# Dilated values with tokens in rows: a stage of their own, two of three head groups by seven block products, read back by class order from DRAM

## The chip, the core and the metric

The kernel runs on one core of one Trainium2 chip. The time is the device time of one execution in microseconds (us). Three runs of the kernel before took 1468.01, 1468.41 and 1469.43 us; their median, 1468.41 us, is what the new time is compared with. A core has five engines that take their instructions in order, each from its own queue: TensorE (PE in the profile, its weight loads PEld), VectorE (DVE), ScalarE (ACT), GpSimd (POOL) and SyncE (SP). SP issues most DMAs here, ScalarE's queue some.

## What is computed

The reference is one layer of an encoder: a normalised input of 1024 tokens x 1024 channels, three mixers beside each other, gates, and an output projection.

```python
h = rms_norm(x, g_pre)
a_qkv, bq, bk, bv, mq, ga, gb, gm, mg = split(h @ w_in)
# A: dilated sliding windows, 3 groups of 8 heads of 64, (window, dilation) = (128,1), (512,4), (2048,16)
aq, ak, av = rope(a_q, pos), rope(a_k, pos), a_v
for gi, (window, dil) in enumerate(A_GROUPS):     # keys and queries regrouped by token % dil
    o_g, lse_g = dilated_window_attention(aq[gi], ak[gi], av[gi], window, dil)
oa = sum over groups of softmax(lse)[g] * o_g
# B: grouped-query attention (8 heads, 2 key heads), M: cross-attention into 256 memory rows
ya, yb, ym = (oa * silu(ga)) @ w_br_a, (ob * silu(gb)) @ w_br_b, (om * silu(gm)) @ w_br_m
merged = sigmoid(mg0)*ya + sigmoid(mg1)*yb + sigmoid(mg2)*ym
out = x + rms_norm(merged @ w_out, g_post)
```

The change concerns `av`, the values of the dilated mixer: 3 groups x 8 heads x 64 = 1536 columns of `h @ w_in`, for 1024 tokens.

## The kernel before

Every large product is made in float32 by three passes of a split operand: `x = xh + xl`, `w = wh + wl`, and `xh*wh + xl*wh + xh*wl`. The input, transposed, stays in SBUF as eight pairs `hh[k]`, `hl[k]` (channels k in partitions, tokens along the row). `split` (L104) makes a pair: ScalarE copies the high part, VectorE subtracts it.

A *unit* is 128 columns of `w_in` for all tokens. `load_w` (L110) loads its 512 KB into one of two `wr` tiles from SP and splits it into one of two pairs `wh`, `wl`; `add_unit` (L195) puts it in a queue: for each half of the tokens 24 matmuls (8 k x 3 passes, lines L143, L145, L147 of `dense`) into one of two PSUM banks `d`, and then an evacuation that frees the bank. The weights stand still, the tokens move, so a unit's result has channels in partitions and tokens along the row. `weave` (L174) merges the matmuls of the queue with the instructions of an attention in one order for TensorE, which is written out by hand; each attention piece has a cost, and pieces and matmuls advance in proportion to what is left. A piece's own instructions come after its cost has been spent in matmuls, so the last piece of an attention item comes behind all matmuls woven with that item. In the stages spoken of here the orders of VectorE, ScalarE, GpSimd and SP are set by a planner of the framework, from priorities and its own costs; some stages fix those by hand too (`manual_schedule`).

The order of the work: the input is split and the cross-attention is made; then the grouped-query attention with gate units woven in (`b_att`); then the dilated stage (PSUM phase `ps_a`); then the 22 merge-gate units that are left, by a block scheme with seven products per pair (phase `ps_w`); then the branch products and the output projection.

The dilated stage works on 12 items, head pairs p = 0..3 by groups g = 0..2, in the order (0,0), (0,1), (0,2), (1,0) and so on. Each item has three units: query, key, value (`add_a`, L869; the very first item has them in the order value, key, query). Queries and keys are rotated by `rope_half` (L851): four VectorE products of 32 partitions into `t2a`, one of 128 into `t1a` (L860, L861), and a GpSimd sum (L867) that also writes tokens regrouped by class (token % dilation). The value evacuation (L892) multiplies by the inverse norm into `vta`, by class too; GpSimd copies the half blocks at the ends of a class into `vda` (L898). While an item's attention runs, the units of the next item are woven in: `weave(3, ...)`.

The attention of an item (`item`, L904; `plan`, L1066) has eight token tiles T of 128 queries. In the order of `plan`: scores of tiles 0 to 3 come at the end of the item before, behind its first half product with the values (`joined(it["pv"][0], nxt["scores"][0])`); softmax of a tile is VectorE's masked minimum (L960) and ScalarE's exponentials; TensorE transposes the weights (L985, L994), ScalarE copies them out (L997); scores of tiles 4 to 7 and the second half product of the item before stand after tile 3; sums of the exponentials are joined on VectorE (L1025, L1028). The products with the values (L1011) need keys in partitions, so `values` (L913) transposes the value tile block by block on TensorE (L925), 9, 12 and 8 blocks for g = 0, 1, 2, and ScalarE copies them into `avs` (L927).

Of the kernel before, what the change touches and what calls it, by code (L numbers as in the profile page):

```python
# [8 lines left out]
F32 = mybir.dt.float32  # L9
R = mybir.dt.float32r  # L10
# [40 lines left out]
def block(ctx: ExitStack, tc: tile.TileContext, x, xT, memT, cst, msk, bcst, tabA, gpost,  # L51
          wu, wb, wmem, wbr, wout, out):
    nc = tc.nc
# [177 lines left out]
    wgd = dram.tile([4, 2, 3, S], F32, name="wgd")  # L231
    tsd = dram.tile([4, 4, P, 512], F32, name="tsd")


# [407 lines left out]


    with tc.tile_pool(name="ba", bufs=1, reuse_waits="tile") as ba:
        fp["p"] = ba
# [24 lines left out]
        def b_const():  # L670
# [5 lines left out]
            for t in nmt:  # L676
                V.memset(t, 0.0)

        half = [slice(0, 512), slice(512, 1024)]

# [138 lines left out]
    close(qp)  # L819
    close(kvp)  # L820
    end_psum()
    phase_psum("ps_a", s1=4, t=2)
# [5 lines left out]
    with tc.tile_pool(name="aa", bufs=1, reuse_waits="tile") as aa:  # L828
# [4 lines left out]
        nc.sync.dma_start(tab, tabA)  # L833
        vd = aa.tile([P, 2, 4, 2, 64], F32, name="vda")
        G.memset(vd, 0.0)
        V.tensor_tensor(tab[:, 0], tab[:, 0], rb, op=OP.mult)
# [32 lines left out]
        def add_a(p_, g):  # L869
            base = (p_ * 3 + g) * 3  # L870
            d = OPS[p_, g] = {}

            def qk_evac(name, scale):
                def evac(half, p):
                    if half == 0:
                        d[name] = ab.tile([P, S], F32, name=f"a{name}", bufs=2)
                    rope_half(d[name], half, p, scale, g)
                return evac

            def v_evac(half, p):  # L880
                if half == 0:
                    d["vt"] = aa.tile([P, S], F32, name="vta", bufs=1)
                vt = d["vt"]
                n = S // DIL[g]
                rv = rb[:, half * 512:half * 512 + 512]
                if g == 0:
                    dst = vt[:, half * 512:half * 512 + 512]
                else:
                    r = DIL[g]
                    dst = vt.rearrange("p (r u) -> p r u", r=r)[:, :, half * (n // 2):(half + 1) * (n // 2)]  # L890
                    p, rv = [v.rearrange("p (u r) -> p r u", r=r) for v in (p, rv)]
                fp["last"] = V.tensor_tensor(dst, p, rv, op=OP.mult)  # L892
                if half == 1 and g < 2:
                    for h in range(2):
                        hs = slice(h * 64, h * 64 + 64)
                        for e in range(2):
                            src = vt[hs].rearrange("p (r u) -> p r u", r=DIL[g])[:, :, e * (n - 64):e * (n - 64) + 64]
                            G.tensor_copy(vd[hs, e, :DIL[g], h], src)  # L898

            units = [(base, qk_evac("q", -0.125)), (base + 1, qk_evac("k", None)), (base + 2, v_evac)]  # L900
            for u, evac in units if base else units[::-1]:
                add_unit(wu[u], evac)

        def item(p_, g):  # L904
# [4 lines left out]
            part = [i for i, b in enumerate(blocks) if b[1] == 64]  # L909
            order = full + part  # L910
            pos = {b: i for i, b in enumerate(order)}

            def values(i0):  # L913
                if i0 == 0:
                    d["vs"] = aa.tile([P, 12, 2, 64], F32, name="avs", bufs=1)
                vs, vt = d["vs"], d["ops"]["vt"]
                grp = order[i0:i0 + 4]
                tp = pst()
                for j, b in enumerate(grp):
                    c, m = blocks[b]  # L920
                    if m == 128:
                        src = vt[:, c:c + m]
                    else:
                        src = vd[:, int(c % (S // DIL[g]) > 0), c // (S // DIL[g])].rearrange("p z u -> p (z u)")
                    PE.transpose(tp[:, j, :], src, ident)  # L925
                n = len(grp)
                A.activation(vs[:, i0:i0 + n].rearrange("p b h d -> p b (h d)"), tp[:, :n], AF.Copy)  # L927

# [42 lines left out]
            def trans(T):  # L971
                lo, hi, mo = window(g, T)
                n = hi - lo
                pr = st[T]
                kb = blocks_of(T)
                tp = pst()
                pp = aa.tile([P, 4, 128], F32, name="app", bufs=6)
                terms = [[], []]

                def add(slot, h, i):  # L980
                    terms[h].append((pos[i], h, pp[:, slot]))
                if n == 192:
                    f, e = [[b[0] for b in kb if b[2] == m][0] for m in (128, 64)]
                    for slot, c in enumerate((0, 256, 128)):
                        PE.transpose(tp[:, slot, :], pr[:, c:c + 128], ident)  # L985
                    for h in range(2):
                        add(h, h, f)
                        add(2, h, e)
                    k = 3
                else:  # L990
                    k = 0
                    for i, c, m in kb:
                        for h in range(2):
                            PE.transpose(tp[:, k, :], pr[:, h * n + c:h * n + c + 128], ident)  # L994
                            add(k, h, i)
                            k += 1
                A.activation(pp[:, :k], tp[:, :k], AF.Copy)  # L997
                st[T] = terms

            def pv(b):  # L1000
                if b == 0:
                    d["og"] = OG[p_, g] = cb.tile([P, S], F32, name="og", bufs=4)
                og, vs = d["og"], d["vs"]
                ov = pst().rearrange("p a b -> p (a b)")
                for j in range(4):
                    terms = st.pop(4 * b + j)
                    n = len(terms[0])
                    for i in range(n):
                        for h in range(2):
                            x, z, pp = terms[h][i]  # L1010
                            PE.matmul(ov[h * 64:h * 64 + 64, j * 128:j * 128 + 128], vs[:, x, z], pp,  # L1011
                                      start=i == 0, stop=i == n - 1)
                if g == 0:
                    dst, src = og[:, b * 512:b * 512 + 512], ov
                else:
                    r = DIL[g] // 2
                    dst = og.rearrange("p (u r) -> p r u", r=DIL[g])[:, b * r:b * r + r]
                    src = ov.rearrange("p (r u) -> p r u", r=r)
                A.activation(dst, src, AF.Copy)

            def stats():
# [32 lines left out]
                key=(p_, g),  # L1054
                values=[(lambda i0=i0: values(i0), 109.0 * len(order[i0:i0 + 4])) for i0 in range(0, len(order), 4)],
                scores=[(lambda b=b: scores(b), 350 + sum(size[4 * b:4 * b + 4]) * 4 / 2.4) for b in range(2)],
# [9 lines left out]
        def plan(it, pre, nxt):  # L1066
# [116 lines left out]

        half = [slice(0, 512), slice(512, 1024)]

        def first_blocks():
# [394 lines left out]
GATES_A = ((0, 1), (0, 2), (0, 3))  # L1581
U_G = 36
U_MQ = 48
U_M = 52


def layout(inp):
# [13 lines left out]
    for p in range(4):  # L1601
        for g in range(3):
            b = (g * 8 + 2 * p) * 64
            units += [unit(1536 * j + b + np.arange(128)) for j in range(3)]
    for i in range(3):
# [4 lines left out]
    for j in range(24):  # L1610
        units.append(unit(7424 + 128 * j + np.arange(128)))
    r['wu'] = c(np.stack(units)).reshape(len(units), P, 1024)

    i16 = np.arange(16)
# [52 lines left out]

_ORDER = ['x', 'xT', 'memT', 'cst', 'msk', 'bcst', 'tabA', 'gpost', 'wu', 'wb', 'wmem', 'wbr', 'wout']

# [18 lines left out]
```

## Time and profile before

| | |
|---|---|
| median of three runs | 1468.41 us (1468.01 to 1469.43) |
| profiled execution | 1470.83 us, its span 1469.1 us |
| mean granted TensorE clock | 0.996 |
| TensorE busy | 1444.6 us, 98% of the span |
| VectorE, ScalarE, GpSimd busy | 65%, 43%, 34% |
| DMA | 147.07 MB, mean 100 GB/s |

The page of the profile shows busy time by engine, the span in 40 slices with the granted clock, the DMA queues, the chain of work that ended last, and the costliest groups of instructions. A group's row gives line, engine, operation, names (`out<-in`), shape and count, then busy time in us and mean ns of one, then the idle time of the engine ahead of them and who ended it. Busy time of a matmul overlaps its successor's, so the pace of matmuls is read from the starts in the timeline (start and duration in us, then engine, line, operation). A table by windows gives, for each stretch, its length, the busy time of each engine with its instruction count, and at the end the granted clock (1.00 is full), the busy share of the DMA engines, and GB/s.

### The profile page before, as it was taken

To read this page: it belongs to the slowest core of one execution; us is meant where nothing else is said; L and a number is where in the kernel's file an instruction comes from. 1 tells how busy PE (TensorE), PEld (TensorE's weight loads), DVE (VectorE), ACT (ScalarE), POOL (GpSimd) and SP (SyncE) were. 2 spreads that over 40 slices of the span, in tenths; PEclk is the share of its full clock that TensorE was granted. 3 is DMA by queue.
4 is the path that set the end of the run, shared out by engine and by line. 5 is a ranking of instruction groups with operands and counts; after the bars stand their busy time and mean duration, and the time that the engine had idled before them with its cause. 6 is when DMAs were issued, how large, how long until landed. Compare 5 with 4: busy or idle time off the path is not lost.

```text
span 1469.1 us, 20897 instructions
## 1 busy us (share of the span) xinstructions
PE 1444.6 (98%) x7712; PEld 1159.9 (79%) x7712; DVE 961.9 (65%) x1687; ACT 627.2 (43%) x1405; POOL 504.2 (34%) x398
## 2 busy tenths in 40 slices
PE   7999999999999999999999999999999999999998
PEld 7899986666666888888888888888888888887887
DVE  7765468677772666556655755673888787579643
ACT  6544365665554144443443534454534434212221
POOL 1425405566565332123223322321234331044322
PEclk9999999999999999999999999999999999999999
DMA  6332022222111211112112111331443443797122
GB/s 237 103 112 73 30 67 83 77 97 83 65 60 47 93 32 42 30 46 73 58 44 75 45 44 46 88 101 66 160 144 129 173 172 133 255 291 267 71 94 101
DMA packets 66854, 147.07 MB, mean 100 GB/s; under 512 B 15104, under 2 KB 25024, under 8 KB 66624
## 3 DMA queue, kind: packets, MB, share of 16 engines
q1 hardware_dynamic: 60272, 134.07, 28.4%
q10 hardware_dynamic: 6480, 11.67, 2.2%
q8 instruction: 60, 0.98, 0.3%
q14 instruction: 42, 0.34, 0.1%
HBM read 111.79 MB, written 33.91 MB: 99 GB/s over the span
## 4 chain that ended last, share of the span: by engine, by line
PE 84%; DVE 5%; DMA 3%; ACT 3%; issue 2%; POOL 2%; SPq 0%; POOLq 0%; ACTq 0%; DVEq 0%
PE s L125 14%; PE d L143 12%; PE d L147 12%; PE d L145 12%; PE sc L125 6%; PE sc L1539 5%; PE ov L743 3%; PE tr L1011 3%; PE s L948 2%; DMA raw<-rld 2%; PE d L534 2%; PE s L728 2%; PE s L727 2%; PE tr L709 2%; PE tr L994 1%
## 5 line engine op out<-in xcount | busy, mean ns | idle before, releaser
L143 PE MATMUL d<-hh,wh 128*128 128x512 f32 x864 | 345.6, 400 | 1.7 <-DVE fth L222 1.7
L147 PE MATMUL d<-hh,wl 128*128 128x512 f32 x864 | 346.7, 401 | 0.0
L145 PE MATMUL d<-hl,wh 128*128 128x512 f32 x864 | 342.2, 396 | 0.0
L143 PEld LDWEIGHTS d<-hh,wh 128*128 128x128 f32 x864 | 162.8, 188 | 42.9 <-issue 7.6
L147 PEld LDWEIGHTS d<-hh,wl 128*128 128x128 f32 x864 | 162.7, 188 | 35.9 <-issue 5.2
L145 PEld LDWEIGHTS d<-hl,wh 128*128 128x128 f32 x864 | 162.7, 188 | 34.8 <-issue 4.5
L105 ACT ACTIVATE wh<-wr 128x1024 fp32r<-128x1024 f32 (+1 forms) x89 | 83.8, 943 | 245.1 <-PE d L145 148.3
L734 POOL TENSOR_TENSOR bl<-bl,bp 128x512 f32<-128x512 f32 x96 | 130.7, 1362 | 60.8 <-ACT bp L730 55.2
L125 PE MATMUL sc<-hh,wh 128*128 128x512 f32 x384 | 121.0, 396 | 2.7 <-DVE wh L106 2.3
L867 POOL TENSOR_TENSOR aq<-t1a,t2a 128x512 f32<-128x512 f32 x24 | 54.5, 2271 | 163.6 <-DVE t1a L861 163.6
L861 DVE SCALAR_TENSOR_TENSOR t2a<-d,tab 32x512 f32<-32x512 f32 x96 | 66.0, 687 | 62.8 <-PE d L147 61.8
L106 DVE TENSOR_TENSOR wl<-wr,wh 128x1024 fp32r<-128x1024 f32 x65 | 85.4, 1315 | 28.2 <-ACT wh L105 28.2
L867 POOL TENSOR_TENSOR ak<-t1a,t2a 128x512 f32<-128x512 f32 x24 | 55.1, 2296 | 117.5 <-DVE t1a L860 117.5
L710 DVE TENSOR_REDUCE bn<-tr 128x1 f32<-128x512 f32 x128 | 85.6, 683 | 14.4 <-PE tr L709 13.6
L730 ACT ACTIVATE bp<-s 128x512 f32<-128x512 f32 x128 | 75.6, 594 | 45.6 <-PE s L728 44.7
L125 PEld LDWEIGHTS sc<-hh,wh 128*128 128x128 f32 x384 | 73.3, 191 | 18.8 <-DVE wh L106 2.8
L860 DVE TENSOR_TENSOR t2a<-d,tab 32x512 f32<-32x512 f32 x96 | 66.0, 687 | 24.9 <-PE d L147 21.2
L1468 POOL TENSOR_TENSOR acc<-acc,th 128x1024 f32<-128x1024 f32 x15 | 41.0, 2731 | 117.1 <-DVE th L1467 114.8
L1260 POOL TENSOR_TENSOR sf<-wr 128x512 f32<-128x512 f32 x22 | 30.4, 1402 | 140.8 <-DVE ch L106 61.4
L960 DVE CUSTOM_DVE_ANT_0 pra<-s,mask 128x192 f32<-128x192 f32 (+2 forms) x192 | 56.8, 348 | 32.3 <-PE s L948 23.8
L125 PE MATMUL sc<-hl,wh 128*128 128x512 f32 x192 | 75.7, 394 | 0.0
L968 ACT ACTIVATE pra<-pra,sts 128x128 f32<-128x128 f32 (+2 forms) x152 | 66.5, 439 | 19.6 <-DVE sts L960 19.6
(317 smaller groups left out, 3113.4 us busy)
## 6 DMA issues: line engine op xcount, KB each, us to landing
wr<-in_wu SPq DMA_DIRECT2D x76, 512.0 KB
th<-thd SPq DMA_DIRECT2D x24, 512.0 KB
thd<-rs ACTq DMA_DIRECT2D x44, 256.0 KB
g2d<-fth SPq DMA_DIRECT2D x24, 256.0 KB
wgt<-wgd SPq DMA_DIRECT2D x24, 256.0 KB
ot<-od SPq DMA_DIRECT2D x12, 512.0 KB
wr<-in_wbr SPq DMA_DIRECT2D x24, 256.0 KB
wr<-in_wmem SPq DMA_DIRECT2D x8, 512.0 KB
```

Of the source, the lines that this page charges most:

```text
L105: A.activation(dst_h, src, AF.Copy)
L106: V.tensor_tensor(dst_l, src, dst_h.bitcast(F32), op=OP.subtract)
L125: PE.matmul(out_ps, a, b, start=i == 0, stop=i == n - 1)
L143: PE.matmul(dst, wh[:, k, :], hh[k][:, t], start=k == 0, stop=False)
L145: PE.matmul(dst, wh[:, k, :], hl[k][:, t], start=False, stop=False)
L147: PE.matmul(dst, wl[:, k, :], hh[k][:, t], start=False, stop=k == 7)
L710: fp["last"] = V.tensor_reduce(st[i]["n"][:, j, c:c + 1], s, axis=AX.X, op=OP.min)
L730: A.activation(pp, s, AF.Exp, scale=-1.0)
L734: G.tensor_tensor(lsum[i % 2], lsum[i % 2], pp, op=OP.add)
L867: G.tensor_tensor(half_of(o, half, g), classes(t1, g), classes(t2, g), op=OP.add)
L968: A.activation(src, raw, AF.Exp, scale=-1.0, bias=bias, accum_out=sts[:, h, 1, T:T + 1])
L1539: PE.matmul(parts[h], *terms[h][j], start=j == 0, stop=j == 23)
```

## The change

The value units leave the queue. A new stage stands between the grouped-query attention and the dilated stage, with TensorE's order and those of ScalarE, VectorE, GpSimd and SP written out by hand. There the tokens stand still (128 at a time) and 512 columns of weights move, so that the result has tokens in partitions. The 1536 columns are three groups of 512. The group with dilation 16 is made directly: 16 steps (2 token halves x 8 k) of 12 matmuls. The groups with dilations 1 and 4 together are a product of 2 x 2 blocks, made by seven block products instead of eight, 28 steps of 12 matmuls: sums of weight blocks are made on GpSimd, sums of token blocks (`tsd`, which the kernel before has in DRAM for its later block stage) are loaded, and sums of products are made on VectorE. ScalarE multiplies by the inverse norm and stores to a DRAM tensor `vdr[g, p, token, 128]` on its own queue. The first weights are loaded and split during the last unit of the grouped-query stage (`first_values`), the first unit of the dilated stage during the end of the new one.

In the dilated stage each item has two units (query, then key; the first item too), and `weave(2, ...)`. `values` is no TensorE work any more: it loads the value blocks of an item from `vdr`, by class, into two tiles that all items share, `vfull` (blocks of 128 keys) and `vpart` (half blocks, the other half zero), with 3, 5 or 2 DMAs from SP. `plan` puts it after tile 3, behind the second half product of the item before.

```diff
+    vdr = dram.tile([3, 4, S, 128], F32, name="vdr")
...
-        early[len(queue)] = lambda: load_w(wu[2])
+        early[len(queue)] = first_values
...
+    phase_psum("ps_v", s1=6)
+    v_first = ready.pop(len(queue))
+    manual = tc.manual_schedule(engines={ET.Activation, ET.DVE, ET.Pool, ET.SP})
...
+    PRODUCTS = (("A11", "B11"), ("A12", "B21"), ("S2", "T2"), ("S3", "T3"), ("S4", "B22"), ("S1", "T1"), ("A22", "T4"))
...
+    def v_store(r, g, T, src):
+        A.activation(r, src, AF.Copy, scale=rcol[:, T:T + 1])
+        nc.scalar.dma_start(vdr[g, :, T * 128:T * 128 + 128].rearrange("p t f -> t p f"),
+                            r.rearrange("t (p f) -> t p f", p=4))
...
+    steps_v = [(None, e, k) for e in range(2) for k in range(8)] + [(i, 0, k) for i in range(7) for k in range(4)]
+    for n, (i, e, k) in enumerate(steps_v):
+        if k == 0:
+            now = v_banks()
+        for j in range(4):
+            if i is None:
+                t = slice(e * 512 + j * 128, e * 512 + j * 128 + 128)
+                (bh, bl), w, end = (hh[k][:, t], hl[k][:, t]), v_first[k], 7
+            else:
+                (bh, bl), w, end = tokens_at(i, k, j), SB[i, k], 3
+            wh_, wl_ = parts_of(w)
+            for q, (a, b) in enumerate(((bh, wh_), (bl, wh_), (bh, wl_))):
+                PE.matmul(now[j], a, b, start=k == 0 and q == 0, stop=k == end and q == 2)
+        behind = left.pop(0)() if left else []
...
+            split_at(*divmod(m, 4))
...
-            base = (p_ * 3 + g) * 3
+            base = (p_ * 3 + g) * 2
...
-            units = [(base, qk_evac("q", -0.125)), (base + 1, qk_evac("k", None)), (base + 2, v_evac)]
-            for u, evac in units if base else units[::-1]:
-                add_unit(wu[u], evac)
+            add_unit(wu[base], qk_evac("q", -0.125))
+            add_unit(wu[base + 1], qk_evac("k", None))
...
+                v = vdr[g, p_]
+                if g == 2:
+                    vv = v.rearrange("(u r) f -> u r f", r=16)
+                    for z in range(2):
+                        nc.sync.dma_start(vfull[z * 64:z * 64 + 64].rearrange("p b h d -> p b (h d)"), vv[:, z::2])
+                    return
+                if g == 0:
+                    nc.sync.dma_start(vfull[:, 0:7].rearrange("p b h d -> p b (h d)"),
+                                      v[64:960].rearrange("(b q) f -> q b f", q=128))
...
-                PE.transpose(tp[:, j, :], src, ident)
...
-                if it and 4 <= T < 4 + len(it["values"]):
-                    out += [(lambda: None, 300.0), it["values"][T - 4]]
...
                 if T == 3:
                     out.append(joined(pre and pre["pv"][1], it and it["scores"][1]))
+                    if it:
+                        out.append((it["values"], 0.0))
...
-        weave(3)
+        weave(2)
...
-            weave(len(GATES_A) if last else 3, run(pieces), sum(c for _, c in pieces), 1.0)
+            weave(len(GATES_A) if last else 2, run(pieces), sum(c for _, c in pieces), 1.0)
```

More of the change, by code (lines that the diff above doesn't have):

```diff
@@ L641, in block, with first_values @@
     phase_psum("ps_b", s1=2, t=3, o=1)
+    def first_values():
+        hl_ = []
+        for i in range(2):
+            raw = wp.tile([P, 1024], F32, name="wr", bufs=WR)
+            nc.sync.dma_start(raw.rearrange("p (k f) -> p k f", k=2), wv[VG[0], :, 2 * i:2 * i + 2])
+            hl_ += [(raw[:, half[j]], wp.tile([P, 1024], R, name=("wh", "wl")[j])) for j in range(2)]
+        for raw, t in hl_:
+            split(t[:, half[0]], t[:, half[1]], raw)
+        return [t for _, t in hl_]
+    half = [slice(0, 512), slice(512, 1024)]
     with tc.tile_pool(name="ba", bufs=1, reuse_waits="tile") as ba:
@@ new lines, in block, with rs @@
+    slots0 = [slot() for _ in range(4)]
+    def rs():
+        return vp.tile([P, 512], F32, name="vr", bufs=8)
+    raw1 = vp.tile([P, 4, 512], F32, name="sum1")
+    for i in range(2):
+        nc.sync.dma_start(raw1[:, 2 * i:2 * i + 2], wv[VG[0], :, 4 + 2 * i:6 + 2 * i])
+    VR = {}
+    for nm, u, kh in (("A21", 1, 0), ("A11", 0, 0), ("A22", 1, 1), ("A12", 0, 1)):
+        VR[nm] = vp.tile([P, 4, 512], F32, name=f"v{nm}")
+        for i in range(2):
+            nc.sync.dma_start(VR[nm][:, 2 * i:2 * i + 2], wv[VG[1 + u], :, 4 * kh + 2 * i:4 * kh + 2 * i + 2])
@@ new lines, in block, with parts_of, blocks_at @@
+    VR.update(S1=raw1, S3=VR["A21"], S2=VR["A11"], S4=VR["A12"])
+    vv = [vp.tile([P, 512], F32, name=f"vv{j}") for j in range(4)]
+    vy = [vp.tile([P, 512], F32, name=f"vy{j}") for j in range(4)]
+    SB, TB_ = {}, {}
+    def parts_of(t):
+        return t[:, lo], t[:, hi]
+    def blocks_at(i, k):
+        an, bn = PRODUCTS[i]
+        if bn[0] != "T":
+            return
+        w = k < 2 and i in (3, 5)
+        SB[i, k], TB_[i, k] = (wslot(0), wslot(1)) if w else (slot(), slot())
+        nc.sync.dma_start(TB_[i, k][:, hi].bitcast(F32), tsd[int(bn[1]) - 1, k])
@@ new lines, in split_at, with tokens_at @@
+    def split_at(i, k):
+        an, bn = PRODUCTS[i]
+        if (i, k) not in SB:
+            SB[i, k] = wslot(k % 2) if i == 1 else slot()
+        split(*parts_of(SB[i, k]), VR[an][:, k])
+        if bn[0] == "T":
+            h, l = parts_of(TB_[i, k])
+            split(h, l, l.bitcast(F32))
+    def tokens_at(i, k, j):
+        bn = PRODUCTS[i][1]
+        c = slice(j * 128, j * 128 + 128)
+        if bn[0] == "T":
+            return [x[:, c] for x in parts_of(TB_[i, k])]
+        kk, t = k + 4 * (bn[1] == "2"), (lo, hi)[bn[2] == "2"]
+        return [x[kk][:, t][:, c] for x in (hh, hl)]
@@ L821, in block @@
+    for f in left:
+        for g in f():
+            g()
+    manual.__exit__(None, None, None)
+    close(vpp)
     end_psum()
@@ L980, in add @@
                 def add(slot, h, i):
-                    terms[h].append((pos[i], h, pp[:, slot]))
+                    terms[h].append((place[i], h, pp[:, slot]))
                 if n == 192:
@@ L1054, in item @@
                 key=(p_, g),
-                values=[(lambda i0=i0: values(i0), 109.0 * len(order[i0:i0 + 4])) for i0 in range(0, len(order), 4)],
+                values=values,
                 scores=[(lambda b=b: scores(b), 350 + sum(size[4 * b:4 * b + 4]) * 4 / 2.4) for b in range(2)],
@@ L1603, in layout @@
             b = (g * 8 + 2 * p) * 64
-            units += [unit(1536 * j + b + np.arange(128)) for j in range(3)]
+            units += [unit(1536 * j + b + np.arange(128)) for j in range(2)]
     for i in range(3):
```

136 lines of the change are left out of this document (90 added, 46 removed).

## The prediction

> **What bounds the kernel now.** I read the page's head first, then busy time by stage over the stage of the dilated attention (which I call the dilated stage), then the groups of TensorE instructions in it.
>
> ```profile
> span 1469.1 us, 20897 instructions
> PE 1444.6 (98%) x7712; PEld 1159.9 (79%) x7712; DVE 961.9 (65%) x1687; ACT 627.2 (43%) x1405; POOL 504.2 (34%) x398
> ```
> ```profile
> sum 554.40, PE 554.01 PEld 450.54 DVE 336.13 ACT 229.78 POOL 151.89; mean PE 92.34 PEld 75.09 DVE 56.02 ACT 38.30 POOL 25.31
> ```
> ```profile
> L925 PE MATMUL tr<-cs,vta 128*128 128x128 f32 x76 | 11.5, 272 | 0.0
> L925 PE MATMUL tr<-cs,vda 128*128 128x128 f32 x40 | 7.0, 272 | 0.0
> ```
>
> The second fence is the sum line from 473.6 to 1028 us, the dilated stage: TensorE is busy 554.01 of 554.40 us, VectorE 61% of it. So here the time is the number of TensorE instructions times their pace, and any wait that TensorE gets is new time. The timeline gives the paces.
>
> ```profile
> 490.10 0.39 PE L143 MATMUL d<-hh,wh 128*128 128x512 f32 x1
> ...
> 498.26 0.39 PE L143 MATMUL d<-hh,wh 128*128 128x512 f32 x1
> ...
> 517.94 0.60 PE L994 MATMUL tr<-cs,pra 128*128 128x128 f32 x4
> ```
>
> Between the first two rows lie 36 matmuls of 512 columns: 8.16 us / 36 = 0.227 us each. Four transposes take 0.60 us, one alone 0.27: 0.11 us for each further one.
>
> **What goes.** Twelve value units of 48 matmuls (576) become 16 steps of 12 for the first head group and 28 steps of 12 for the other two, 528 in all: 48 x 0.227 = 10.9 us gained. The 76 + 40 value transposes go: 116 x 0.11 = 12.8 us. Together 23.7 us, all on the path. The value evacuations on VectorE, the copies on ScalarE and GpSimd go too; none holds TensorE up, so they count nothing.
>
> **What is late next: keys at the item boundary.** Before, an item's units run query, key, value, and the next item's first scores come behind the value unit:
>
> ```profile
> 539.03 3.07 POOL L867 TENSOR_TENSOR ak<-t1a,t2a 128x512 f32<-128x512 f32 x1 [4.00 <-DVE t1a L860]
> ...
> 547.10 1.97 PE L1011 MATMUL tr<-app,avs 128*64 128x128 f32 x32
> ...
> 593.44 1.16 PE L948 MATMUL s<-ak,aq 64*128 64x128 f32 x16
> ...
> 633.90 1.09 PE L1011 MATMUL tr<-app,avs 128*64 128x128 f32 x16
> ...
> 634.93 1.89 PE L948 MATMUL s<-ak,aq 64*128 64x192 f32 x16
> ```
>
> The second half of the keys is ready at 542.10; the products with the values start at 547.10 and the scores behind them 1.90 us later. That lead is the value unit. Without it the last dense matmul before a boundary belongs to the second half of the key unit itself; then come only the products with the values, then scores that read this half. TensorE takes its instructions in order, so nothing covers the rotary step. Its price, from the first units of the stage:
>
> ```profile
> 494.02 1.29 POOL L867 TENSOR_TENSOR ak<-t1a,t2a 128x512 f32<-128x512 f32 x1 [3.62 <-DVE t1a L860]
> ...
> 506.19 0.39 PE L147 MATMUL d<-hh,wl 128*128 128x512 f32 x1
> 506.69 2.79 DVE L861 SCALAR_TENSOR_TENSOR t2a<-d,tab 32x512 f32<-32x512 f32 x4 [2.01 <-PE d L147]
> 509.51 0.69 DVE L861 SCALAR_TENSOR_TENSOR t1a<-d,tab 128x512 f32<-128x512 f32 x1
> 510.28 2.18 POOL L867 TENSOR_TENSOR aq<-t1a,t2a 128x512 f32<-128x512 f32 x1 [4.23 <-DVE t1a L861]
> ...
> 547.03 1.06 ACT L105 ACTIVATE wh<-wr 128x1024 fp32r<-128x1024 f32 x1 [7.41 <-PE d L145]
> 548.30 1.22 DVE L106 TENSOR_TENSOR wl<-wr,wh 128x1024 fp32r<-128x1024 f32 x1
> ...
> 577.86 1.68 DVE L1025 TENSOR_TENSOR sts<-sts,lxa 128x4 f32<-128x4 f32 x1 [0.51 <-ACT pra L965]
> ```
> ```profile
> L960 DVE CUSTOM_DVE_ANT_0 pra<-s,mask 128x192 f32<-128x192 f32 (+2 forms) x192 | 56.8, 348 | 32.3 <-PE s L948 23.8 <-PE tr L985 4.7 <-PE tr L994 3.3
> ```
>
> Count from the start of the last dense matmul (506.19). VectorE begins at 0.50 and needs 3.51 us for its five instructions; in the new order a weight split of 1.22 us, released by that same matmul, stands among them; the GpSimd sum starts 0.08 later and takes 2.18 (1.29 for the first head group, whose order is contiguous). Keys are ready at 0.50 + 3.51 + 1.22 + 0.08 + 2.18 = 7.5 us. TensorE arrives at 0.23 + 1.90 = 2.1.
> - Into the second head group, 4 boundaries: 7.5 - 2.1 = 5.4 us idle each, 21.6.
> - Into the third, 4 boundaries: the finished item's two L1025 sums (up to 1.68 each) wait for its last exponentials and now stand ahead of the rotary steps of both key halves. Ends 5.4 and 5.4 + 3.4 = 8.8; I take 7.5, nearer the upper, since only a unit's half (24 x 0.227 = 5.4 us) lies between. 30.0.
> - Into the first, 3 boundaries: only the fourth token tile needs the second half, TensorE arrives at 0.23 + 1.03 + 1.1 = 2.4 (three quarters of 8 scores). But four softmax steps of 0.35 us stand between the halves of the rotary step: 0.50 + 3.51 + 1.22 + 1.4 + 0.08 + 1.29 = 8.0. 5.6 each, 16.8.
>
> Sum 68.4 us. If the split or the sums fell elsewhere it would be 4.2 a boundary (46); with all of them late, and 1 us more of backlog, 82.
>
> **The clock.** Such gaps cost twice; the trace has two gaps to price it:
>
> ```profile
> 52.98 0.50 PE L143 MATMUL d<-hh,wh 128*128 128x512 f32 x1 [1.69 <-DVE fth L222]
> ...
> 1326.62 0.39 PE L125 MATMUL sc<-hl,wh 128*128 128x512 f32 x1
> 1329.34 1.22 PE L125 MATMUL sc<-hh,wh 128*128 128x512 f32 x2 [2.33 <-DVE wh L106]
> ```
> ```profile
> 54.00:55.00 1.00, 1.00 (x6) 0.82 (x5) 1.00 (x3) 0.00 (x0) 0.35 (x1) 1.00 0.89 217
> ...
> 1328.00:1329.00 1.00, 0.00 (x0) 0.00 (x0) 1.00 (x2) 0.96 (x1) 0.23 (x1) 0.76 0.19 78
> ...
> 1335.00:1336.00 1.00, 1.00 (x5) 0.83 (x4) 1.00 (x2) 0.00 (x0) 1.00 (x1) 0.82 0.00 0
> ```
>
> The third number from the end is the granted clock. After 1.69 us idle it stays at 1.00. After 2.33 us it is at half from 1328.5 (0.76 of that slice) to 1335.4, 6.0 us of it behind the gap: 3.0 us lost. Here each gap is over twice as long, so I count a drop at every one. If the slow stretch has its 6.8 us from 1.5 us into the gap whatever follows, 3.0 us of it lie behind a gap of 5.4: 1.5 lost. Between 1.5 and 3.0 I take 2.2; with the gap at the stage's start (below) 12 x 2.2 = 26.4 us.
>
> [...]
>
> **Start of the new stage and of the dilated stage.**
>
> ```profile
> 473.98 0.69 DVE L212 TENSOR_TENSOR fth<-d,rb 128x512 f32<-128x512 f32 x1 [2.24 <-PE d L147]
> ...
> 479.35 0.32 SPq L817 DMA_DIRECT2D rld<-rl  x1
> ```
> ```profile
> 487.13 3.27 POOL L837 TENSOR_TENSOR tab<-tab,rb 128x1024 f32<-128x1024 f32 x1
> ```
> ```profile
> 486.87 1.26 DVE L836 TENSOR_TENSOR tab<-tab,rb 128x1024 f32<-128x1024 f32 x1
> ```
> ```profile
> 271.20 3.72 DMA tx<-in_xT
> ...
> 1291.49 12.46 DMA raw<-rld
> ```
> ```profile
> L106 DVE TENSOR_TENSOR ch<-sf,ch 128x512 fp32r<-128x512 f32 x44 | 36.9, 838 | 20.7 <-ACT ch L105 20.7
> L1283 DVE TENSOR_TENSOR rs<-s,sp 128x512 f32<-128x512 f32 x44 | 30.0, 683 | 1.9 <-PE s L125 1.9
> L1260 POOL TENSOR_TENSOR sf<-sf,wr 128x512 f32<-128x512 f32 x11 | 21.6, 1961 | 0.1
> ```
>
> The grouped-query stage ends near 473.6. SP can issue the new stage's weight loads only behind its last store (479.35). Ahead of it the first four blocks need two loads and four half splits where one load and one split stood, beside the last unit of that stage. The fifth block is due after four steps, at 473.6 + 10.9 = 484.5, and comes at 479.7 + 3.72 + about 1.5 of splitting = 484.9; I take 1 us. A step is 12 x 0.227 = 2.7 us; VectorE's most in one is two splits and two sums, 1.7 + 1.4 = 3.1, in two steps near the end that have two steps of lead; a GpSimd sum of 1.96 fits. So the block products cost nothing beside TensorE. Their stores lie on ScalarE's queue, where nothing waits for them until the dilated stage.
>
> At the head of the dilated stage the query unit is now first (before, values were, which need no rotary table). Its evacuation stands on VectorE behind the split of the third unit, which waits for a weight slot that the query unit holds to its end: 48 x 0.227 = 10.9, + 1.06 + 1.22 (split), + 1.26 (table), + 3.51 (rotary) = 17.9. The key unit wants that PSUM bank at 10.9: 7.0 idle, plus 0.7 at the first item's fourth tile: 7.7 us. If the table alone held it (landing and 3.27 on GpSimd), it might be 4; with late loads 10.
>
> The class-order loads (40 DMAs on SP, 12 + 20 + 8 over the groups) wait for the previous item's second product with the values. Until the first product needs them TensorE has 1.5 + 44 x 0.227 + 12 x 0.11 = 12.8 us of work. A load of 512 KB takes 3.72 us undisturbed, 256 KB in the busiest stretch 12.46; they stay hidden. The weight load queued behind them on SP is due about 13 us later, hidden too.
>
> **Sum.** -23.7 + 68.4 + 26.4 + 1 + 7.7 = +79.8 us. The profiled execution took 1470.83 us (span 1469.1), 2.4 above the median of the three runs, 1468.41. On the median: 1548.
>
> **Rivals.**
> - *Keys are in time, the kernel is faster.* One place decides: the boundary. The change wins if a boundary costs less than (23.7 - 8.7) / 11 = 1.4 us, so if keys were ready 3.5 us after the last dense matmul. Free boundaries give 1468.4 - 23.7 + 8.7 + 2.2 = 1456. For it: VectorE has 39% slack. Against: the rotary step alone has 0.50 + 3.51 + 1.29 = 5.3 us in the rows, with no queue ahead. 0.05.
> - *The clock holds.* Gaps stay but the rate does not drop: 1548 - 26 = 1522. For it the row at 52.98, against it the one at 1329.34, the nearer in length. 0.10.
> - *Value loads are late.* At 12.46 us and more behind other waits on SP they would hold the products ahead of the scores; only what exceeds the key wait is added, say 3 us at 11 boundaries: 1581. Against it 12.8 us of cover. 0.08.
> - *The block products lose their gain* to waits for loads (5 MB of weights in 40 us): +11, 1559. 0.04.
>
> My forecast has 0.68; 0.05 remains for a VectorE backlog beyond 1590. The range runs from the low terms (46 + 18 + 4 - 23.7 = +44, 1512) to the high ones (82 + 36 + 10 + 3 + 10 of waits inside items - 23.7 = +117, 1586): 1508 to 1588, and holds the clock, load and product cases too. Within 0.2% of before is what a measurement of this kernel can't tell from no change: 0.01; faster 0.05; slower 0.94.
>
> **What would show it.** Right: TensorE waiting on GpSimd's key sum in the score line, 11 gaps of 5 to 8 us some 36 to 40 us apart; granted clock below 1.00 behind each; one gap of 7 us about 131 us after the grouped-query stage, behind the table and the third split; no value transposes; a new stage of 120 us without gaps. Wrong: gaps under 2 us at the boundaries, or a clock of 1.00 behind them; products waiting on a DMA; TensorE idle inside the block products.

## The result, and the profile after

The changed kernel takes 1541.56 us (1541.41 to 1542.29, four runs) beside 1468.53 us for the kernel before (1468.01 to 1469.43, four runs on the same chip): 1.0497 times as long, 95% interval 1.0484 to 1.0509. It is slower by 73.0 us; 79.8 were forecast. The profiled execution took 1542.29 us, its span is 71.4 us above that of before.

The head of the page, then TensorE's list of waits (engine, tile and line that waited, who released it, us in total, times, longest):

```profile
span 1540.5 us, 20847 instructions
...
PE 1446.4 (94%) x7548; PEld 1158.2 (75%) x7548; DVE 989.4 (64%) x1731; ACT 644.4 (42%) x1441; POOL 495.9 (32%) x382
```
```profile
PE s L1097 <- POOL ak L1030: 59.4, 12, 5.9
PE d L143 <- DVE t1a L1024: 9.1, 1, 9.1
...
PE tr L1134 <- ACT app L1146: 1.8, 3, 0.8
```

TensorE is busy 94% of the span instead of 98%. The first line is the wait that the prediction named: scores (L1097 now) behind GpSimd's sum of the keys (L1030 now). Of its twelve waits eleven are boundaries, 58.5 us; the twelfth is 0.9 us inside the first item. The second line is the start of the dilated stage. Together the three lines make 70.3 us of idle time. One boundary, into the second group, from the timeline of four engines:

```profile
656.92 0.39 PE L147 MATMUL d<-hh,wl 128*128 128x512 f32 x1
...
657.72 1.48 PE L1160 MATMUL tr<-app,avs 128*64 128x128 f32 x24
664.43 2.93 PE L1097 MATMUL s<-ak,aq 64*128 64x192 f32 x16 [5.23 <-POOL ak L1030]
```
```profile
657.41 1.37 DVE L1023 TENSOR_TENSOR t2a<-d,tab 32x512 f32<-32x512 f32 x2 [1.26 <-PE d L147]
658.82 1.22 DVE L106 TENSOR_TENSOR wl<-wr,wh 128x1024 fp32r<-128x1024 f32 x1
660.07 1.40 DVE L1023 TENSOR_TENSOR t2a<-d,tab 32x512 f32<-32x512 f32 x2
661.50 0.69 DVE L1023 TENSOR_TENSOR t1a<-d,tab 128x512 f32<-128x512 f32 x1
```
```profile
662.27 2.10 POOL L1030 TENSOR_TENSOR ak<-t1a,t2a 128x512 f32<-128x512 f32 x1 [3.89 <-DVE t1a L1023]
```

The chain is the one counted: the last dense matmul, two of VectorE's rotary products, the split of a weight, the rest of the rotary step, GpSimd's sum, the scores. Keys are there 7.45 us after the start of the last dense matmul; 7.5 was said. The stages, by windows (length, busy time of PE, PEld, DVE, ACT, POOL with counts, granted clock, DMA share, GB/s); the second fence is the work behind the dilated stage in the kernel before:

```profile
473.70:593.50 119.80, 119.80 (x530) 99.22 (x529) 54.05 (x76) 44.44 (x74) 22.54 (x17) 1.00 0.39 127
593.50:1102.14 508.64, 438.29 (x2615) 351.38 (x2613) 308.23 (x726) 202.77 (x645) 121.30 (x59) 0.92 0.24 69
...
1102.14:1540.50 438.36, 428.70 (x1910) 354.62 (x1908) 316.23 (x375) 143.70 (x263) 132.71 (x79) 1.00 0.49 167
```
```profile
1028.25:1469.10 440.85, 431.36 (x1910) 356.74 (x1908) 314.33 (x375) 143.82 (x263) 132.13 (x79) 0.99 0.49 166
```

The new stage has no gap: 119.80 us for 528 matmuls, 0.227 us each. The dilated stage has the idle time and a mean clock of 0.92. Summed over slices of half a microsecond, the half clock behind the twelve gaps takes 29.3 us. The account of the span: -23.7 (work that went) + 70.3 (idle) + 29.3 (clock) - 2.5 (the last stage, where before has a slow stretch that is missing here) = 73.4, measured 71.4.

### The profile page after: what moved, and what is told of

It reads as the page before. It is cut to its first block, busy times and chain, and to the rows that moved or that the text cites. A ratio compares the mean times of both kernels' runs of the same rounds, so it can differ in the third digit from the quotient of the medians.

```text
span 1540.5 us, 20847 instructions
## 1 busy us (share of the span) xinstructions
PE 1446.4 (94%) x7548; PEld 1158.2 (75%) x7548; DVE 989.4 (64%) x1731; ACT 644.4 (42%) x1441; POOL 495.9 (32%) x382
## 3 DMA queue, kind: packets, MB, share of 16 engines
q1 hardware_dynamic: 76528, 144.56, 29.3%
## 5 line engine op out<-in xcount | busy, mean ns | idle before, releaser
L143 PE MATMUL d<-hh,wh 128*128 128x512 f32 x672 | 277.2, 412 | 10.8 <-DVE t1a L1024 9.1
L145 PE MATMUL d<-hl,wh 128*128 128x512 f32 x672 | 273.5, 407 | 0.0
L147 PE MATMUL d<-hh,wl 128*128 128x512 f32 x672 | 273.0, 406 | 0.0
L143 PEld LDWEIGHTS d<-hh,wh 128*128 128x128 f32 x672 | 130.1, 194 | 46.0 <-issue 17.4
L105 ACT ACTIVATE wh<-wr 128x1024 fp32r<-128x1024 f32 (+1 forms) x79 | 72.2, 917 | 212.5 <-PE d L145 122.2
L145 PEld LDWEIGHTS d<-hl,wh 128*128 128x128 f32 x672 | 130.6, 194 | 30.3 <-issue 6.8
L147 PEld LDWEIGHTS d<-hh,wl 128*128 128x128 f32 x672 | 129.7, 193 | 30.0 <-issue 4.8
L1030 POOL TENSOR_TENSOR aq<-t1a,t2a 128x512 f32<-128x512 f32 x24 | 54.4, 2268 | 186.0 <-DVE t1a L1024 160.2
L1097 PE MATMUL s<-ak,aq 64*128 64x192 f32 (+2 forms) x384 | 48.6, 402 | 59.4 <-POOL ak L1030 59.4
L1109 DVE CUSTOM_DVE_ANT_0 pra<-s,mask 128x192 f32<-128x192 f32 (+2 forms) x192 | 56.3, 348 | 72.0 <-PE s L1097 52.6
L106 DVE TENSOR_TENSOR wl<-wr,wh 128x1024 fp32r<-128x1024 f32 x53 | 74.2, 1401 | 38.2 <-ACT wh L105 37.8
L1097 PEld LDWEIGHTS s<-ak,aq 64*128 64x128 f32 x384 | 37.4, 236 | 66.7 <-POOL ak L1030 62.9
L125 PEld LDWEIGHTS sc<-hh,wh 128*128 128x128 f32 x384 | 72.0, 188 | 16.8 <-DVE wh L106 1.9
L1030 POOL TENSOR_TENSOR ak<-t1a,t2a 128x512 f32<-128x512 f32 x24 | 43.9, 1828 | 120.5 <-DVE t1a L1023 113.9
```

The costliest lines, as they stand in the source:

```text
L105: A.activation(dst_h, src, AF.Copy)
L106: V.tensor_tensor(dst_l, src, dst_h.bitcast(F32), op=OP.subtract)
L125: PE.matmul(out_ps, a, b, start=i == 0, stop=i == n - 1)
L143: PE.matmul(dst, wh[:, k, :], hh[k][:, t], start=k == 0, stop=False)
L145: PE.matmul(dst, wh[:, k, :], hl[k][:, t], start=False, stop=False)
L147: PE.matmul(dst, wl[:, k, :], hh[k][:, t], start=False, stop=k == 7)
```

## The experiments

The theory: a score that reads the unit made last must wait for that unit's rotary step; in the changed kernel this is the key unit at every boundary, and each such gap is paid a second time in clock. Rivals: VectorE's amount of work, the loads of values or the two-unit items cause the waits; the clock falls for another reason.

**The queue shifted by one unit.** The same units, but three are woven ahead of the first item, so that the next item's key unit ends a unit earlier.

```diff
-        weave(2)
+        weave(3)
...
-            weave(len(GATES_A) if last else 2, run(pieces), ...
+            weave(2, run(pieces), ...
```

> The unit queue is shifted by one unit: three units are woven ahead of the first item, so that the unit ahead of a boundary is the query unit of the item after next, and the key unit has ended 10.9 us (48 x 0.227) before the boundary. The work is the same; the last item has two gate units beside it, the one before it one key and one gate unit. Theory (TensorE waits for the rotary step of the last key half): the 11 waits on the key sum go (58.5 us in the trace of the changed kernel, and 0.9 inside the first item), and with them the half clock behind each (26.5 us): 1541.6 - 85.9 = 1456 us, the wait of 9.1 us at the start of the dilated stage stays. Rival A (a full queue of VectorE, which does the same work in either order, holds the boundary): the waits move to the masked minimum of the first tiles, and the time stays above 1520. Rival B (values read by class order are late as well, and the key wait hides it): waits on a DMA appear in the products with the values; 1480 to 1500.

Measured: 1465.47 us beside 1470.3 for before, ratio 0.9965 (0.9944 to 0.9987). All waits on the key sum are gone, and the kernel is a little faster than before, by 0.35%. TensorE's waits that belong to the change's stages:

```profile
PE d L143 <- DVE t1a L1024: 9.1, 1, 9.1
...
PE tr L1179 <- ACT app L1146: 4.6, 6, 1.4
PE tr L1134 <- ACT app L1146: 2.8, 4, 1.6
```

Both rivals fall: no wait on VectorE's masked minimum, none on a DMA. The profiled execution, the fastest of the five, took 1463.4 us, 7 above the 1456 expected: 5.6 of them are new waits, short ones, of transpositions for ScalarE's copies, which neither theory had.

**The key unit ahead of the query unit.** (In this run the very first key unit is made with the query unit's weights, since their load is written out elsewhere; the number, size and order of the loads and instructions stay as described.)

```diff
-            add_unit(wu[base], qk_evac("q", -0.125))
             add_unit(wu[base + 1], qk_evac("k", None))
+            add_unit(wu[base], qk_evac("q", -0.125))
```

> In each item the key unit is queued ahead of the query unit, and nothing else is changed. Theory (it is the rotary step of whatever half is last, where a score reads that half): into the first head group, whose tokens stay in order, tiles 0 to 3 read the first half of the queries alone, so its three waits go (15.5 us, and 5.8 us of half clock behind them) and the 0.9 inside the first item; into the second and third group, regrouped by class, the queries of the first tiles lie in both halves, and the eight waits stay: 1541.6 - 22 = 1519 us. Rival A (only late keys matter): all 11 waits go, 1456. Rival B (the wait comes from the change of items itself, the products with the values or VectorE's backlog, not from the unit that is last): no change, 1541.

Measured: 1517.96 us, ratio 1.0328 (1.0300 to 1.0357), as the theory had it (1519), against 1456 and 1541 of the rivals. The waits have changed their tile:

```profile
PE s L1097 <- POOL aq L1030: 40.5, 11, 5.0
```

They are 4.7 to 4.8 us into the second group, behind scores of one tile that need the first half alone (three of them wait 0.4 to 0.5 us more), and 5.0 into the third. None is left into the first group. So it isn't the keys as such, nor the change of items, but any half that is last and is read at once.

**The gaps filled with work that nobody reads.**

```diff
+        def fill():
+            bank = pst().rearrange("p a b -> p (a b)")
+            for i in range(22):
+                PE.matmul(bank, hh[i % 8][:, 0:128], hh[i % 8][:, 0:512], ...)
...
-                    out.append(joined(it["pv"][0], nxt and nxt["scores"][0]))
+                    out.append(joined(it["pv"][0], nxt and (fill, 0.0), nxt and nxt["scores"][0]))
```

> The change is kept as it is, and 22 matmuls of 512 columns (22 x 0.227 = 5.0 us) whose result nobody reads are put behind the products with the values at each of the 11 boundaries, ahead of the scores. The keys come as late as before, so TensorE cannot go on earlier, but it is idle for at most 1 us. Theory (the gaps cost twice, the second time by the clock behind them): the granted clock stays at 1.00 at the boundaries, and the 26.5 us of half clock behind them go: 1515 us, with waits on the key sum of 0 to 1 us each. Rival (the clock falls for another cause, such as the load of the stage): the clock is as before and the time is 1541 or, with some of the filling on the path, more.

Measured: 1520.48 us, ratio 1.0341 (1.0318 to 1.0364). The stage's mean clock is back at 0.99, though TensorE can go on with the scores no earlier than before:

```profile
593.50:1082.00 488.50, 472.86 (x2867) 378.57 (x2866) 307.65 (x729) 202.34 (x648) 122.86 (x59) 0.99 0.25 71
```
```profile
658.67 5.28 PE L1218 MATMUL tr<-hh 128*128 128x512 f32 x22
664.01 1.57 PE L1097 MATMUL s<-ak,aq 64*128 64x192 f32 x16
```

The span is 22.1 us shorter. Filling and scores are 5.34 us apart (58.7 in 11), and 2.0 us of waits for the keys are left at the boundaries, for 58.5 us of gaps; other short waits grew by 1.5. The clock alone is therefore worth about 22.1 + 2.2 + 1.5 = 25.8 us. About 1 us of it belongs to the gap at the start of the stage, which is in both runs (1.8 us of half clock behind it here, 2.8 in the changed kernel); the rest, some 25 us, stands beside the 26.5 expected of the eleven boundaries. It was the gaps that brought the clock down.

**The weight split behind the rotary step.** In the dilated stage a unit's split is ordered behind the last product of the rotary step queued before it (`fp["last"]`), which is meant to take its 1.22 us out of the chain.

```diff
-        split(wh[:, :n], wl[:, :n], raw[:, :n])
+        if behind_rotary:
+            with tc.issue_after(fp["last"].ins):
+                split(wh[:, :n], wl[:, :n], raw[:, :n])
...
+        behind_rotary.append(True)
```

> The weight split of the dilated stage's units is ordered behind the rotary step whose instructions it stood between, on VectorE and ScalarE; all else is as in the change. Theory (the chain counted in the prediction: rotary step, weight split of 1.22 us, GpSimd's sum): each of the 11 gaps is 1.2 us shorter, 4.6 instead of 5.9 us into the second group: 13.4 us. For the clock there are two readings: a slow stretch of a fixed length behind a gap, then 1541.6 - 13.4 = 1528 us; or one of a fixed length from 1.5 us into the gap, then each us of gap that goes comes back as half a us of slow work, 6.7 us in all, and the time is 1535 us. Rival (the split is not on that path, since GpSimd or the bank holds it): 1541.

Measured: 1535.1 us, ratio 1.0439 (1.0415 to 1.0463); the span is 8.7 us shorter. The waits on the key sum fell from 59.4 to 53.5 us, not by 13.4: 5.2 to 5.9 became 4.85 us into the second group, and the others lost 0.3 to 0.4 only. VectorE and GpSimd at one boundary:

```profile
773.19 0.69 DVE L1029 TENSOR_TENSOR t1a<-d,tab 128x512 f32<-128x512 f32 x1
773.80 1.21 DVE L106 TENSOR_TENSOR wl<-wr,wh 128x1024 fp32r<-128x1024 f32 x1
```
```profile
773.96 3.01 POOL L1036 TENSOR_TENSOR ak<-t1a,t2a 128x512 f32<-128x512 f32 x1 [1.42 <-DVE t1a L1029]
```

The split now starts just ahead of the sum, and the sum takes 3.01 us instead of 2.10: 0.9 of the 1.2 us come straight back (below). So the split was in the chain, but its price isn't freed by moving it there. The time lies at the second of the two clock readings (1535), yet not for its reason: the half clock behind the gaps fell a little, from 29.3 to 26.8 us, where that reading had it rise by 6.7. Neither reading holds.

**The kernel before, with the key unit last.**

```diff
-            units = [(base, qk_evac("q", -0.125)), (base + 1, qk_evac("k", None)), (base + 2, v_evac)]
+            units = [(base, qk_evac("q", -0.125)), (base + 2, v_evac), (base + 1, qk_evac("k", None))]
...
```

> The kernel before, with the value unit of each item queued between its query and its key unit instead of behind them, so that the key unit is the last before a boundary (to keep the single value tile free, an item's value transposes and the second half product of the item before stand some tiles earlier). Nothing of the change is in it: no new stage, no loads of values, three units an item. Theory (the place of the key unit alone makes the waits): 11 waits on the key sum of 5 us and the half clock behind each (2.2 us): 1468.5 + 11 x 7.3 = 1549 us. Rival (it is the two units an item, the value loads or the new stage that bring the waits): 1468 to 1478, with the waits that the moved pieces may give.

Measured: 1553.28 us, ratio 1.0564 (1.0544 to 1.0583), 1549 expected. Without a new stage or a load of values, the old kernel shows the same gaps:

```profile
PE s L948 <- POOL ak L867: 56.3, 11, 5.2
```
```profile
547.35 0.39 PE L147 MATMUL d<-hh,wl 128*128 128x512 f32 x1
547.67 1.97 PE L1011 MATMUL tr<-app,avs 128*64 128x128 f32 x32
554.85 0.69 PE L948 MATMUL s<-ak,aq 64*128 64x192 f32 x2 [5.21 <-POOL ak L867]
```

The span rose by 82.6 us: 56.3 idle and 26.3, or 2.4 a gap, for the clock and small waits. The pieces that had to move with the unit bring no wait of that size of their own. The place of the key unit is enough to explain the loss.

**Shifted queue, and the rotary table loaded early.** The table goes into a tile of its own during the block products; the first three units have their orders written out, so that the third unit's split comes behind the first rotary step.

```diff
+    rtab = tb.tile([P, 2, S], F32, name="rtab")
...
+        if n == FIRST + 8:
+            nc.sync.dma_start(rtab, tabA)
...
-        V.tensor_tensor(tab[:, 0], tab[:, 0], rb, op=OP.mult)
+            V.tensor_tensor(tab[:, 0], rtab[:, 0], rb, op=OP.mult)
...
-        weave(2)
+        with tc.manual_schedule(engines={ET.Activation, ET.DVE, ET.Pool}):
+            weave(3)
```

> As the shifted queue, and the start of the dilated stage is changed: the rotary table is loaded during the block products into a tile of its own, multiplied by the inverse norm as soon as the new stage ends, and the first three units have the orders of VectorE, ScalarE and GpSimd written out, so that the split of the third unit comes behind the query unit's rotary step. Theory (table and split hold the second PSUM bank at the start): the table product can run by 597, the query's first half is rotated by 604, before TensorE comes back to the bank; the wait of 9.1 us and the 1.9 us of half clock behind it go: 11 us below the shifted queue, 1452 us where before has 1468.5 (the shifted queue had 0.9965 of before, 1463.4). Rival A (the table alone, or the split alone, held it): half of it stays, 1457. Rival B (the 1 MB load of the table collides with the loads of the block products): waits of 1 to 5 us in the new stage, 1454 to 1457.

Measured: 1452.44 us beside 1468.8, ratio 0.9889 (0.9871 to 0.9907); 1452 expected. TensorE is busy 98% of the span again, and the wait of 9.1 us is gone:

```profile
span 1450.7 us, 20862 instructions
...
PE 1419.5 (98%) x7548; PEld 1137.0 (78%) x7548; DVE 984.8 (68%) x1731; ACT 641.4 (44%) x1441; POOL 497.6 (34%) x382
```
```profile
598.04 1.21 DVE L1002 TENSOR_TENSOR tab<-rtab,rb 128x1024 f32<-128x1024 f32 x1
```

The account of this span against before: -23.7 + 7.2 (short waits for ScalarE's copies) - 2.4 (last stage) = -18.9, measured -18.4. So the 23.7 us that the change takes away are real. Which of the two, table or split, would have held the bank alone was not tried; in the changed kernel both came free within half a us of each other (below).

**The statistics one tile later**, on top of that.

```diff
-                if T == 2 and pre:
+                if T == 3 and pre:
                     out += [(lambda: None, 300.0), pre["stats"]]
```

> As the run with the early table, and the transposition of a finished item's statistics stands one tile later in TensorE's order, ahead of the scores of tiles 4 to 7 of the next item instead of behind its second softmax. In the shifted queue's trace six of these transpositions waited for ScalarE's copies, 4.6 us in all. Theory (with 96 dense matmuls in an item instead of 144 ScalarE has less time between pieces): these waits go, 4.6 us, 1447 to 1448 us. Rival (ScalarE's copy is late wherever the next reader of that PSUM tile stands): the wait passes to the next transposition and the time is that of the run with the early table.

Measured: 1451.88 us, ratio 0.9880 (0.9864 to 0.9895), not to be told from the run above. The rival was right: the waits of these transpositions fell from 4.4 to 1.0 us and those of the others rose from 2.8 to 4.6. It is the lowest median of the study, 16.9 us below before.

**All three head groups made directly**, on top of the early table: 48 steps instead of 44, no sums.

```diff
-    steps_v = [(None, e, k) for e in range(2) for k in range(8)] + [(i, 0, k) for i in range(7) for k in range(4)]
+    steps_v = [(u, e, k) for u in range(3) for e in range(2) for k in range(8)]
...
```

> As the run with the early table, but all three head groups are made directly, 48 steps of 12 matmuls (576) instead of 44 (528), without sums of weight or token blocks. Theory (the block products have all of their gain, since everything else is hidden beside TensorE): 48 x 0.227 = 10.9 us above the run with the early table, 1463 us. Rival (the seven products lose part of the gain to loads or sums): less than 6 us above it.

Measured: 1465.2 us, ratio 0.9971 (0.9960 to 0.9981), 12.8 above the run with block products.

```profile
473.60:604.86 131.26, 131.26 (x580) 108.33 (x578) 20.81 (x27) 30.59 (x47) 3.31 (x2) 1.00 0.34 114
```
```profile
605.92 0.50 PE L143 MATMUL d<-hh,wh 128*128 128x512 f32 x1 [1.06 <-ACT vr L902]
```

The stage is 11.5 us longer, and a wait of 1.06 us for a PSUM bank follows it. The seven products kept all of their gain.

## Why the prediction was right, and where its sizes were off

The mechanism, its place and its sign were right; the time is 6.4 us below the forecast, within the range. That it is so near is in part luck: 9.9 us too much into the third group stand against 6.4 too little into the second, for the clock and at the start. By its own steps:

- *What goes, -23.7 us:* right, by the stage's length and by the account of the run with the early table.
- *Into the second group, 5.4 us each:* 5.23 once and 5.87 three times, 22.8 in all against 21.6. The split takes up to 1.88 us where it runs beside GpSimd's sum of the first half.
- *Into the third group, 7.5 us each:* wrong, 5.0 each, 20.1 instead of 30.0. This is the term that was mis-sized. The sum at L1025 took its 1.68 us beside a sum of GpSimd's and ended with that, at 579.5; without that neighbour it takes 0.16, and both of the item's sums were over before the second key half came. What is left at this boundary is the chain without them, with a GpSimd sum of 1.89 us:

```profile
577.42 2.09 POOL L867 TENSOR_TENSOR ak<-t1a,t2a 128x512 f32<-128x512 f32 x1 [7.47 <-DVE t1a L860]
```
```profile
690.31 0.16 DVE L1174 TENSOR_TENSOR sts<-sts,lxa 128x4 f32<-128x4 f32 x1 [1.70 <-ACT pra L1114]
692.29 0.16 DVE L1174 TENSOR_TENSOR sts<-sts,lxa 128x4 f32<-128x4 f32 x1 [1.81 <-ACT pra L1114]
...
697.69 1.38 DVE L1023 TENSOR_TENSOR t2a<-d,tab 32x512 f32<-32x512 f32 x2 [1.73 <-PE d L147]
```
```profile
704.50 1.91 PE L1097 MATMUL s<-ak,aq 64*128 64x128 f32 x16 [5.02 <-POOL ak L1030]
```

- *Into the first group, 5.6 us each:* 5.18 each, 15.5 against 16.8, and only the fourth tile waits, as said.
- *The clock, 26.4 us:* 29.3 by the slices for twelve gaps, 26.5 of it at the eleven boundaries; some 25 there by the filled gaps. The two bounds a gap (1.5 and 3.0) were nearly those found (1.6 to 3.2), but not their reason: the loss does not follow the length of the gap.
- *First loads of the new stage, 1 us:* none.
- *Start of the dilated stage, 7.7 us:* 9.1 + 0.9 = 10.0. The place and the order were right; the term for the table was too small. The rotary step needs both halves of the table, VectorE's product and GpSimd's; VectorE's began 0.3 us after GpSimd's and took 3.36 us instead of the 1.26 of before:

```profile
605.52 1.23 DVE L106 TENSOR_TENSOR wl<-wr,wh 128x1024 fp32r<-128x1024 f32 x1 [7.63 <-ACT wh L105]
606.67 3.36 DVE L999 TENSOR_TENSOR tab<-tab,rb 128x1024 f32<-128x1024 f32 x1
```
```profile
606.35 2.60 POOL L1000 TENSOR_TENSOR tab<-tab,rb 128x1024 f32<-128x1024 f32 x1 [17.63 <-DMA tab<-in_tabA]
```

In the run with the filled gaps VectorE came first, and the wait is as long (9.2 us), now by GpSimd's half:

```profile
607.13 1.23 DVE L999 TENSOR_TENSOR tab<-tab,rb 128x1024 f32<-128x1024 f32 x1
```
```profile
607.17 3.38 POOL L1000 TENSOR_TENSOR tab<-tab,rb 128x1024 f32<-128x1024 f32 x1 [18.01 <-DMA tab<-in_tabA]
```

In the changed kernel the table has landed at 606.35 and the split of the third unit ends at 606.75. So the load, which the prediction put at 4 us if it alone held the bank, held it nearly as long as the split.

- *Value loads and block products at nothing:* right; no product waited for a DMA, and the new stage has no gap.
- *The rivals:* keys in time fails at the boundary as worked out. Where a run puts the keys in time, its price of 1456 is roughly borne out: 1465 with the start's wait, 1452 without. A clock that holds fails too, since the clock fell behind each of the twelve gaps; with the gaps filled the time is 1520, where this rival had 1522. Not foreseen were 5.6 us of short waits on ScalarE in the items with two units.

## What to carry to other kernels

A unit taken out of a queue may be the one that covered the latency of the unit ahead of it: look which result the next in-order consumer reads first, and how much work is left between the two. Here a shift of the queue by one unit, two lines, turned +73 us into a kernel 0.35% faster than before, and 1.1% faster with the early table. And a gap of a full-time TensorE should be priced with its clock, a duration in a row with the neighbour that ran beside it.

## What was not expected of the hardware

**The clock changes on a fixed grid.** The 44 times at which the clock fell or rose at the boundaries of the changed kernel and of the run with the moved split fit, in each trace, a grid of 3.413 us to within 0.01 us. Windows cut on that grid (the number behind the counts is the clock): first the boundary that ends at 704.50, then the one that ends at 899.54, one at 1056.82, and the gap of the kernel before that the prediction used.

```profile
697.89:701.30 3.41, 1.59 (x30) 1.34 (x26) 3.32 (x5) 1.65 (x2) 0.25 (x1) 1.00 0.09 17
701.30:704.71 3.41, 0.21 (x2) 0.21 (x4) 1.14 (x2) 0.00 (x0) 1.89 (x1) 1.00 0.53 163
704.71:708.12 3.41, 3.41 (x20) 2.89 (x19) 1.36 (x12) 2.14 (x11) 0.00 (x0) 0.50 0.00 0
708.12:711.54 3.42, 3.42 (x20) 2.68 (x19) 0.51 (x4) 2.04 (x8) 0.00 (x0) 1.00 0.00 0
```
```profile
892.43:895.84 3.41, 1.25 (x24) 1.00 (x20) 3.33 (x4) 0.81 (x2) 1.66 (x1) 1.00 1.06 240
895.84:899.25 3.41, 0.00 (x0) 0.00 (x0) 1.44 (x3) 0.00 (x0) 1.86 (x1) 0.50 1.11 225
899.25:902.67 3.42, 3.13 (x17) 2.69 (x18) 1.45 (x7) 1.05 (x5) 0.24 (x1) 0.50 0.39 136
902.67:906.08 3.41, 3.41 (x19) 2.83 (x20) 3.41 (x8) 2.37 (x12) 0.00 (x0) 1.00 0.00 0
```
```profile
1056.33:1059.74 3.41, 2.92 (x18) 2.60 (x19) 1.67 (x13) 1.90 (x8) 0.44 (x1) 0.50 0.03 12
1059.74:1063.16 3.42, 3.42 (x10) 2.54 (x10) 0.90 (x2) 2.19 (x8) 0.00 (x0) 0.51 0.01 2
1063.16:1066.57 3.41, 3.41 (x19) 2.78 (x18) 1.72 (x6) 1.77 (x6) 0.00 (x0) 1.00 0.00 0
```
```profile
1325.10:1328.52 3.42, 1.54 (x6) 0.64 (x4) 3.32 (x3) 2.17 (x3) 0.00 (x0) 1.00 0.76 293
1328.52:1331.93 3.41, 2.59 (x6) 2.11 (x7) 3.41 (x3) 1.84 (x3) 2.75 (x1) 0.50 0.55 177
```

A window with TensorE busy 1.59 us is followed by full clock, one with 1.54 or 1.25 by half clock: in these traces a little under half of the 3.41 us busy decides, not an idle window as a whole. Back to full speed it went after a window that was busy 3.13 us, not after one of 2.92. No window of the traces of before and of the changed kernel, cut on its grid, contradicts these limits from the first clock record on. So a gap at a boundary cost one slow window or two (3.41 us at two of the eleven boundaries of the changed kernel, 6.83 at nine), and how much of these fell behind the gap hung on where it lay on the grid: 1.6 to 3.2 us lost for gaps of 5 to 6 us. This fits the run with the moved split, where neither reading of the clock held.

**VectorE and GpSimd lengthen each other's instructions.** VectorE's table product starts at 606.67, 0.3 us after GpSimd's, and ends 1.1 us after GpSimd is done (608.95): 3.36 us instead of 1.21 to 1.26. The sum at 577.86 ends with GpSimd's (579.5), 1.68 instead of 0.16. In the run with the moved split VectorE starts 0.16 us first, and it is GpSimd that takes 0.9 more. In the run with the filled gaps VectorE's table product starts 0.04 us first and takes 1.23, and GpSimd's takes 3.38 instead of the 2.40 of the run with the early table, where it stands nearly alone. In each of the four cases the one that starts second takes longer by about the time that the first still needs. The rotary products, which read a PSUM bank, are not lengthened: in the changed kernel two of them take 1.37 us from 657.41, beside a GpSimd sum that runs from 656.23 to 658.38, and two without one take 1.40 us from 660.07. What makes the difference was not tried.
